# A transformer block on one core: u loaded in eleven pieces, q and k at other distances with high and low parts in turn, Fourier weights by parts, k's token scale by way of HBM

## The chip, the cores and the metric

The kernel runs on one core of one Trainium2 chip, which has eight; the other seven have nothing to do. A core has five engines that run side by side, each through its own list of instructions in the order written: PE (matrix products), ACT (element functions), DVE (element arithmetic), POOL (a slower general engine) and SP, which here only starts transfers. They meet at semaphores. The operands lie in an on-chip memory of 128 partitions; matrix products are summed in banks of a second memory, which ACT and DVE read. The metric is the device time of one execution in microseconds (us), shown as the median of several runs.

## The reference

One encoder layer on x of 256 tokens by 2048 features, in float32:

```
h = RMSNorm(x);  q | k | v | u = h @ w_in
a = RMSNorm(window_attention(q, k, v, sink))      12 query heads, 4 key heads, head width 128,
                                                  |t - s| <= 128, linear bias by distance
f = RMSNorm(fourier_mix(u))                       per group of 128 channels: real part of the 2-D
                                                  transform over (positions, channels), then @ w_fourier
x = x + concat(a, f) @ w_out
g | val = RMSNorm(x) @ w_up
x = x + (GELU(conv3(g)) * val) @ w_down           5504 wide
out = RMSNorm(x)
```

The change touches the stage that makes u, q, k and the Fourier part, so the last three lines concern it only as what comes after.

## The kernel before

Every float32 operand that PE multiplies is split in two: `hi`, the value rounded to a format that PE takes in one pass, and `lo`, what is left. A product is then three passes: hi by hi, lo by hi, hi by lo. A copy on ACT makes `hi`, a subtraction on DVE makes `lo`. Weights come in tiles of 1 MB (`raw`, three buffers), are split into `parts` (three buffers, line 152 on) and used; a split is written two units ahead of its use (`split(i + ahead)`, line 379), and a load three ahead. `PLACES` (line 150) says how many elements into its buffer the hi part and the lo part of each kind of tile begin.

**u.** Norm gain, tokens and u's weights come as one array in 16 pieces, one for each 128 features (k). `U_LOADS` (line 187) groups the pieces into nine loads, four of one piece, four of two and one of four. For each load, `u_weights` splits the weights of the whole load at once and `u_tokens` the tokens of each k; then come six matmuls for each k (`u_products`). ACT and DVE do the work of one load in the order: tokens of the first k, weights of the load, tokens of the other k's.

**Units.** After u the program goes through numbered units, each with one weight tile: 4 to 7 are v, 8 to 23 are q and k (k0, q0, q1, q2, k1, q3 ...), 24 to 39 the output projection. `unit(i, work)` (line 395) runs what is registered to come `before` unit i, the unit's own matmuls, what is registered `beside` it, the split of unit i + 2, and what is registered `behind` it. Every entry is placed by hand with `at(when, i, function)`, so the order of each engine's list follows from this. Beside unit 4 stand the squares of the tokens (`token_sums`, eight on ACT) and the token scale r1; beside unit 5 the rows of u, scaled by r1 and split (`rows_out`), and the split of the position cosines `pos`.

**Fourier part.** `fourier_weights` (before unit 6) multiplies the channel cosines `chan` by the weights `wfs`, both plain float32 (line 490, two products which PE takes as two passes each); `fourier_weights_out` copies the result. `fourier_rows` (before unit 7) multiplies u's rows by pos. From unit 8 to 11, `fourier_channels` joins the two for one group each. `total` sums the squares before unit 14.

**k's token scale.** k is kept with features on the partitions, so its scale r1, one number for each token, is needed as a row repeated on all partitions (`r1b`). Behind unit 6 DVE makes two diagonal matrices of r1; before unit 8 PE multiplies them by ones (line 322); beside unit 8 DVE copies the sum to r1b. `qk_out` of k0, beside unit 9, reads it first (line 602).

**q and k.** A unit makes 128 features of q or k for 256 tokens. `still_weights` (line 344) keeps the weights still and moves tokens: for each of 16 k one matmul of the hi weights with 512 columns (hi and lo of the tokens, line 355) and one of the lo weights with 256 (line 357). `lag` says how many further hi matmuls run ahead of the first lo matmul: q and k use 15, all sixteen hi matmuls and then all sixteen lo ones. The feed-forward part uses 0 (in turn), and 4 for its third tile. `qk_parts` splits the result into `kT` and `qT`. Each head then goes through scores, exponentials, transposes and values in the units that follow.

**The feed-forward part** starts at about 270 us with the same `still_weights` for the first tiles and goes on with three matmuls of 256 columns for each k (`still_thirds`, line 361), and with the down projection as a scheme with fewer products.

Of the kernel before, what the change touches and what calls it, by code (L numbers as in the profile page):

```python
# [8 lines left out]
F32 = mybir.dt.float32  # L9
F32R = mybir.dt.float32r  # L10
AF = mybir.ActivationFunctionType
ALU = mybir.AluOpType

P = 128
D = 2048
S = 256
NK = D // P
# [76 lines left out]
def block_kernel(  # L94
# [18 lines left out]
    nc = tc.nc  # L113
    SL = slopes()
    ctx.enter_context(tc.manual_schedule())
    base = ctx.enter_context(tc.tile_pool(name="base", bufs=1))
    wp = ctx.enter_context(tc.tile_pool(name="wp", bufs=1))
    mm = ctx.enter_context(tc.tile_pool(name="mm", bufs=4, space=bass.MemoryType.PSUM))
    dn = ctx.enter_context(tc.tile_pool(name="dn", bufs=4, space=bass.MemoryType.PSUM))

    def f32(ap):
        return ap.bitcast(F32)

    def bank(pool, name):
        return pool.tile([P, 512], F32, tag=pool.name, name=name)
# [21 lines left out]
    raws, halves = {}, {}  # L147


    PLACES = {"qk": (16, 32), "still": (0, 16), "thirds": (0, 32), "first": (16, 16), "moving": (0, 0), "product": (28, 28)}  # L150

    def parts_tile(name, place):
        t = wp.tile([P, 2 * 2048 + 128], F32R, tag="parts", name=name, bufs=3)
        oh, ol = PLACES[place]
        return t[:, oh : oh + 2048], t[:, 2048 + ol : 4096 + ol]
# [27 lines left out]
    def load_u(k, n):  # L183
        s = slice(NK + k * KS if k else 0, NK + (k + n) * KS)
        nc.sync.dma_start(u_raw[:, s], u_in[:, s])

    U_LOADS = [1, 1, 1, 1, 2, 2, 2, 2, 4]
    for n, size in enumerate(U_LOADS):
        load_u(sum(U_LOADS[:n]), size)
    vec = base.tile([P, V_N], F32, tag="vec", name="vec")  # L190
# [16 lines left out]
    ps = bank(dn, "ps_warm")  # L207
# [3 lines left out]
    def split_scaled(dst, src, g):  # L211

        nc.scalar.activation(dst[:, 0:S], src, AF.Copy, scale=g)
        nc.vector.scalar_tensor_tensor(
            dst[:, S : 2 * S], src, g, f32(dst[:, 0:S]), ALU.mult, ALU.subtract
        )

    hT = []
    for c in range(4):
        t = base.tile([P, 4, 512], F32R, tag=f"hT{c}", name=f"hT{c}")  # L220
# [36 lines left out]
    k = 0  # L257
    for size in U_LOADS:
        if k:
# [12 lines left out]
    cat_pool = pa.enter_context(tc.tile_pool(name="cat", bufs=16))  # L272
    ph = pa.enter_context(tc.tile_pool(name="pa", bufs=1))

    chan = cat_pool.tile([P, 512], F32, tag="cat", name="chan")[:, 0 : 2 * P]
    wfs = cat_pool.tile([P, FW], F32, tag="cat", name="wfs")
# [2 lines left out]
    pos_hi = cat_pool.tile([P, 2, S], F32R, tag="cat", name="pos_hi")  # L279
    pos_lo = cat_pool.tile([P, 2, S], F32R, tag="cat", name="pos_lo")  # L280
    rel = cat_pool.tile([P, 512], F32, tag="cat", name="rel")

    nc.sync.dma_start(chan, c_chan)
    nc.sync.dma_start(wfs, wf)
# [26 lines left out]
    def spread_diagonals(r, name):  # L311
        dgs = []
        for b in range(2):
            dg = base.tile([P, P], F32, tag=f"diag{b}", name=f"diag{name}{b}")
            nc.vector.tensor_scalar(dg, ident, r[:, b : b + 1], None, ALU.mult)
            dgs.append(dg)
        return dgs

    def spread_sums(dgs, name):
        ps = bank(dn, "ps_spread" + name)  # L320
        for b in range(2):
            nc.tensor.matmul(
                ps[:, b * P : (b + 1) * P], ones, dgs[b], start=True, stop=True
            )
        return ps
# [18 lines left out]
    def still_weights(hi, lo, ps, kk, lag=0):  # L344


        todo = [("hi", k) for k in kk[: lag + 1]]
        for n, k in enumerate(kk):
            todo.append(("lo", k))
            todo += [("hi", q) for q in kk[lag + 1 + n : lag + 2 + n]]  # L350
        for part, k in todo:
            h = hT[k // 4][:, k % 4, :]
            s = slice(k * P, (k + 1) * P)
            if part == "hi":
                nc.tensor.matmul(ps, hi[:, s], h, start=k == 0, stop=False)  # L355
            else:
                nc.tensor.matmul(  # L357
                    ps[:, 0:S], lo[:, s], h[:, 0:S], start=False, stop=k == NK - 1
                )
# [26 lines left out]
    before, beside, behind = {}, {}, {}  # L386

    def at(when, i, f, *a):
        when.setdefault(i, []).append((f, a))
# [17 lines left out]
    r1 = base.tile([P, 2], F32, tag="rstd1", name="rstd1")  # L407
# [36 lines left out]
    r1b = ph.tile([P, S], F32, tag="r1b", name="r1b")  # L444
# [3 lines left out]
    at(beside, 5, rows_out, u_hi, u_lo, ps_u)  # L448
    at(behind, 5, query_scales)

    cat = {}

    def feature_out(ps, slot, g, sq, first):
# [25 lines left out]

    held = {}  # L480

    def fourier_positions():
        nc.scalar.activation(pos_hi, pos, AF.Copy)
        nc.vector.tensor_tensor(pos_lo, pos, f32(pos_hi), ALU.subtract)

    def fourier_weights():

        for part in range(2):
            ps = held["g", part] = bank(dn, f"ps_g{part}")
            nc.tensor.matmul(  # L490
                ps, chan[:, part * P : (part + 1) * P], wfs, start=True, stop=True
            )

    def fourier_weights_out():
        for part in range(2):
# [28 lines left out]
    sq_f = ph.tile([P, S], F32, tag="sqf", name="sq_f")  # L524
# [30 lines left out]
            nc.vector.tensor_scalar(rel[:, s], rel[:, s], rq_inv[:, b : b + 1], None, ALU.mult)  # L555
        nc.vector.tensor_scalar(sink_neg, vcol(V_SINK, NH), -1.0, None, ALU.mult)

    spread1 = {}
    at(beside, 5, fourier_positions)
    at(before, 6, fourier_weights)  # L560
    at(beside, 6, fourier_weights_out)
    at(behind, 6, lambda: spread1.update(d=spread_diagonals(r1, "1")))
    at(before, 7, fourier_rows)
    at(beside, 7, fourier_rows_out)
    at(before, 8, lambda: spread1.update(ps=spread_sums(spread1["d"], "1")))
    at(beside, 8, lambda: rows_out(v_hi, v_lo, ps_v))
    at(beside, 8, lambda: nc.vector.tensor_copy(r1b, spread1["ps"][:, :S]))
    at(behind, 8, distances)

    def fourier_channels_steps():  # L570
        for g in range(NG):
            i = 8 + g
            at(before, i, fourier_channels, g)
            at(beside, i, fourier_channels_copy, g)
            at(behind, i, fourier_channels_join, g)
            at(beside, i + 1, fourier_channels_out, g)
        at(before, 14, total, sq_f, "f")
        at(beside, 14, total_scale, "f", FW)


# [12 lines left out]
    qk_sb, st = {}, {}  # L593
# [11 lines left out]
    def qk_parts(kind, h):  # L605

        add = st.pop(("add", kind, h))
        t = ph.tile([P, 512], F32R, tag=f"{kind}T", name=f"{kind}T{h}", bufs=2)
        if kind == "k":
            nc.scalar.activation(t[:, 0:S], add, AF.Copy)  # L610
            nc.vector.tensor_tensor(t[:, S : 2 * S], add, f32(t[:, 0:S]), ALU.subtract)
        else:
            split_scaled(t, add, -1.0 / float(SL[h]))
        qk_sb[kind, h] = t
# [91 lines left out]
    for i in range(N_QK, N_OUT + 8):  # L706
        heads = {i - s: h for (kind, h), s in slot_of.items() if kind == "q"}
        new = [kh for kh, s in slot_of.items() if i - s == 1]
        if 5 in heads:
            at(before, i, values, heads[5])  # L710
        if 4 in heads:
            at(before, i, turn, heads[4])
        if 2 in heads:
            at(before, i, scores, heads[2])
        if 3 in heads:
            at(beside, i, weigh, heads[3])
        for kind, h in new:
            at(beside, i, lambda k=kind, h=h: qk_out(k, h, st.pop(("ps", k, h))))
        if 5 in heads:
            at(beside, i, values_out, heads[5])  # L720
        if 4 in heads:
            at(beside, i, turn_out, heads[4])
        for kind, h in new:
            at(beside, i, qk_parts, kind, h)
        if 2 in heads:
            at(beside, i, scores_out, heads[2])
            at(behind, i, exps, heads[2])

    fourier_channels_steps()
    for n, (kind, h) in enumerate(QK_ORDER):  # L730

        def work(hi, lo):
            ps = st["ps", kind, h] = bank(mm, f"ps_{kind}{h}")
            still_weights(hi, lo, ps, range(NK), lag=NK - 1)

        unit(N_QK + n, work)

# [49 lines left out]
    for n, (c, kq) in enumerate(OUT_ORDER):  # L787
        i = N_OUT + n
# [14 lines left out]
        if kq >= 2:  # L803
            part = "a" if kq == 2 else "f"
            ps = ps_a[c] if kq < 3 else ps_a[c, "f"]
# [312 lines left out]
    for q in range(2):  # L1118
        kind, j = items[q]
        ps = bank(mm, f"ps_{kind}{j}")  # L1120
# [16 lines left out]
    for n, it in enumerate(items):  # L1137
# [8 lines left out]
        if it[0] in ("gate", "val"):  # L1146
            kind, j = it
            ps = bank(mm, f"ps_{kind}{j}")
# [7 lines left out]
        if it[0] == "product":  # L1156
            kind, g, c, p = it
            hi, lo = halves.pop(it)
            both = c == 2
            shape = (2, 1024) if both else (4, 512)  # L1160
            for cc in (0, 1) if both else (c,):
                o = 512 * cc if both else 0
                if (cc, p) in held:
                    first, end = (g, c) == FIRST_SET[cc], (g, c) == LAST_SET[cc]
                    by_parts(held[cc, p], parts[p], hi, lo, first, end, *shape, o)
                    continue
                ps = bank(mm, f"ps_{p}{g}{cc}")
# [6 lines left out]
        else:  # L1174
            kind, g, c = it
            hi, lo = halves.pop(up_index[n])
            ps = [bank(mm, f"ps_l{g}{c}{b}") for b in range(2)]
# [10 lines left out]
    i = up_index[n]  # L1188

    def split_last(c):  # L1190
        raw, n = raws[i + c], 512 * len(LAST)
        o = PLACES["product"][0]
        hi, lo = halves[i + c] = [
# [144 lines left out]
```

## Time and profile before

| what | us |
|---|---|
| median of three runs | 947.99 |
| lowest, highest | 947.69, 948.75 |
| the profiled execution | 947.65 |
| its span in the profile | 945.9 |
| PE busy | 936.6 |
| DVE busy | 711.2 |
| ACT busy | 535.7 |
| POOL busy | 47.2 |

The span runs from the first to the last record, 1.75 us less than the execution's own time. The profile gives for each engine when each instruction began and how long it took, with the tiles that it wrote and read and the line of the program; the note in brackets is how long the engine sat idle before, and what released it. An instruction merged over several has an x with their number. PE's matmuls overlap, so the time of one is longer than its share of the stream: the distance from one start to the next is what counts. PEld is the loading of weights into the array, ahead of the matmul that uses them. PEclk is the granted clock of PE as a share of full speed. In the chain of waits, each piece is a stretch of the work that ended last, and its lengths add up without overlap.

### The profile page before, as it was taken

What the parts mean: (1) busy time and instruction counts of PE and PEld (TensorE: products, weight loads), DVE (VectorE), ACT (ScalarE), POOL (GpSimd) and SP (SyncE); (2) the same over time, 40 slices, a digit from 0 to 9 for tenths busy, and PEclk for the clock granted to TensorE, in tenths of its full rate; (3) what the DMA queues carried; (4) which work ended last, traced back from release to release, by engine and by line L of the source; (5) the groups of instructions that cost most, each with busy time, mean ns of one, the idle gap of its engine ahead of it and who ended that gap; (6) DMA issues with size and microseconds to landing.
All of it is one profiled execution on the core that took longest, in us unless ns stands there. A gap on an engine that the chain in (4) does not pass through costs nothing.

```text
span 945.9 us, 15007 instructions
## 1 busy us (share of the span) xinstructions
PE 936.6 (99%) x6277; PEld 858.0 (91%) x6277; DVE 711.2 (75%) x816; ACT 535.7 (57%) x620; POOL 47.2 (5%) x62
## 2 busy tenths in 40 slices
PE   9999999999999999999999999999999999999996
PEld 7889899888888899999999999999999999999985
DVE  6658877666667776769676887768878678889695
ACT  7656666544465555546555555555555555655544
POOL 0000000000000000000000000000000000000003
PEclk9999999999999999999999999999999999999998
DMA  9844534455559687577888778787878987769742
GB/s 365 332 166 160 178 135 153 158 179 181 185 215 299 199 256 227 190 252 223 267 239 257 244 248 266 249 278 224 265 234 239 290 262 248 242 222 261 227 181 89
DMA packets 32260, 214.87 MB, mean 227 GB/s; under 512 B 3520, under 2 KB 3776, under 8 KB 7744
## 3 DMA queue, kind: packets, MB, share of 16 engines
q1 hardware_dynamic: 28160, 184.55, 53.4%
q0 software_dynamic: 4032, 29.36, 16.2%
q8 instruction: 49, 0.80, 0.3%
q14 instruction: 19, 0.16, 0.0%
HBM read 211.80 MB, written 2.10 MB: 226 GB/s over the span
## 4 chain that ended last, share of the span: by engine, by line
PE 96%; DMA 2%; SPq 0%; ACT 0%; DVE 0%; issue 0%; POOL 0%; ACTq 0%; POOLq 0%
PE ps_val L368 22%; PE ps_gate L368 21%; PE ps_q L355 5%; PE ps_P L1061 3%; PE ps_P L1060 3%; PE ps_P L1059 3%; PE ps_N L1060 3%; PE ps_N L1061 3%; PE ps_N L1059 3%; PE ps_q L357 2%; PE ps_a L340 2%; PE ps_a L338 2%; PE ps_a L339 2%; PE ps_gate L355 2%; PE ps_val L355 2%; PE ps_k L355 2%
## 5 line engine op out<-in xcount | busy, mean ns | idle before, releaser
L171 DVE TENSOR_TENSOR parts<-raw,parts 128x2048 fp32r<-128x2048 f32 (+1 forms) x129 | 293.4, 2274 | 70.8 <-ACT parts L170 70.6
L170 ACT ACTIVATE parts<-raw 128x2048 fp32r<-128x2048 f32 (+1 forms) x129 | 245.9, 1906 | 79.5 <-PE ps_gate L368 19.9
L368 PEld LDWEIGHTS ps_val<-hU,parts 128*128 128x128 f32 x1824 | 211.6, 188 | 2.2
L368 PE MATMUL ps_val<-hU,parts 128*128 128x256 f32 x1824 | 212.9, 276 | 0.0
L368 PEld LDWEIGHTS ps_gate<-hU,parts 128*128 128x128 f32 x1776 | 206.4, 188 | 2.5
L368 PE MATMUL ps_gate<-hU,parts 128*128 128x256 f32 x1776 | 207.3, 276 | 0.0
L836 ACT ACTIVATE fa_v<-ps_val 128x256 f32<-128x256 f32 x38 | 14.6, 384 | 88.4 <-PE ps_val L368 88.2
L946 DVE TENSOR_TENSOR parts_N<-sumw,parts_N 128x2048 fp32r<-128x2048 f32 x18 | 41.2, 2290 | 21.2 <-ACT parts_N L945 21.1
L1059 PE MATMUL ps_P<-parts_P,op_P 128*128 128x512 f32 x144 | 56.0, 389 | 0.0
L1061 PE MATMUL ps_P<-parts_P,op_P 128*128 128x512 f32 x144 | 56.0, 389 | 0.0
L1060 PE MATMUL ps_P<-parts_P,op_P 128*128 128x512 f32 x144 | 56.0, 389 | 0.0
L355 PE MATMUL ps_q<-hT,parts 128*128 128x512 f32 x192 | 46.3, 393 | 0.0
L945 ACT ACTIVATE parts_N<-sumw 128x2048 fp32r<-128x2048 f32 x18 | 34.4, 1913 | 14.3 <-PE ps_gate L368 10.6
L1061 PE MATMUL ps_N<-parts_N,op_N 128*128 128x512 f32 x108 | 42.0, 389 | 0.0
L1059 PE MATMUL ps_N<-parts_N,op_N 128*128 128x512 f32 x108 | 42.0, 389 | 0.0
L1060 PE MATMUL ps_N<-parts_N,op_N 128*128 128x512 f32 x108 | 42.0, 389 | 0.0
L355 PEld LDWEIGHTS ps_q<-hT,parts 128*128 128x128 f32 x192 | 35.2, 188 | 6.9
L338 PE MATMUL ps_a<-parts,cat 128*128 128x512 f32 x96 | 37.9, 394 | 0.0
L340 PE MATMUL ps_a<-parts,cat 128*128 128x512 f32 x96 | 37.5, 390 | 0.0
L339 PE MATMUL ps_a<-parts,cat 128*128 128x512 f32 x96 | 37.4, 389 | 0.0
L946 DVE TENSOR_TENSOR parts_P<-sumw,parts_P 128x2048 fp32r<-128x2048 f32 x9 | 20.6, 2289 | 16.6 <-ACT parts_P L945 16.6
L355 PE MATMUL ps_gate<-hU,parts 128*128 128x512 f32 x96 | 32.7, 390 | 0.0
(343 smaller groups left out, 1492.0 us busy)
## 6 DMA issues: line engine op xcount, KB each, us to landing
raw<-in_w_up SPq DMA_DIRECT2D x86, 1024.0 KB, 5.9
raw<-in_w_in SPq DMA_DIRECT2D x20, 1024.0 KB, 4.9
sumw<-in_w_down POOLq DMA_DIRECT2D x18, 1024.0 KB, 8.5
raw<-in_w_out SPq DMA_DIRECT2D x16, 1024.0 KB, 4.9
raw<-in_w_down_late SPq DMA_DIRECT2D x4, 1024.0 KB, 6.2
u_raw<-in_u_in SPq DMA_DIRECT2D x4, 768.0 KB, 9.1
raw<-in_w_down_last SPq DMA_DIRECT2D x4, 768.0 KB, 4.4
xs<-in_x SPq DMA_DIRECT2D x4, 512.0 KB, 17.3
```

The costliest lines, as they stand in the source:

```text
L170: nc.scalar.activation(hi, raw, AF.Copy)
L171: nc.vector.tensor_tensor(lo, raw, f32(hi), ALU.subtract)
L338: nc.tensor.matmul(ps, ah, wh, start=first and q == q0, stop=False)
L339: nc.tensor.matmul(ps, al, wh, start=False, stop=False)
L340: nc.tensor.matmul(ps, ah, wl, start=False, stop=last and q == q0 + len(kk) - 1)
L355: nc.tensor.matmul(ps, hi[:, s], h, start=k == 0, stop=False)
L368: nc.tensor.matmul(ps[:, 0:S], w[:, s], h[:, o : o + S], start=k == 0 and n == 0, stop=k == NK - 1 and n == 2,)
L945: nc.scalar.activation(hi, src, AF.Copy)
L946: nc.vector.tensor_tensor(lo, src, f32(hi), ALU.subtract)
L1059: nc.tensor.matmul(ps, o[:, 0, p, :], hi[:, s], start=first and p == 0, stop=False)
L1060: nc.tensor.matmul(ps, o[:, 1, p, :], hi[:, s], start=False, stop=False)
L1061: nc.tensor.matmul(ps, o[:, 0, p, :], lo[:, s], start=False, stop=end)
```

## The change

Six edits, all in the first 170 us of the span:

- u comes in eleven loads: six of one piece, five of two.
- The hi part of a q or k tile begins 32 elements into its buffer in place of 16, the lo part 80 in place of 32. Units alternate between a lead of four hi matmuls (8, 10, ...) and strictly in turn (9, 11, ...).
- `chan` and `wfs` are split on ACT and DVE beside unit 5, after u's rows and ahead of pos; `fourier_weights` becomes three one-pass matmuls for each of its two products.
- r1 is written by POOL's queue to a row in HBM, behind unit 5, and read back to all partitions as r1b. The diagonals, their two products and the copy go.
- A small tile of 16 elements is set aside after the first `kT`, so that `qT` and what is allocated after it lie 64 bytes further on.
- The call that places `total` before unit 14 stands in another loop.

```diff
-    PLACES = {"qk": (16, 32), "still": (0, 16), "thirds": (0, 32), "first": (16, 16), "moving": (0, 0), "product": (28, 28)}
+    PLACES = {"qk": (32, 80), "still": (0, 16), "thirds": (0, 32), "first": (16, 16), "moving": (0, 0), "product": (28, 28)}
...
-    U_LOADS = [1, 1, 1, 1, 2, 2, 2, 2, 4]
+    U_LOADS = [1] * 6 + [2] * 5
...
+    chan_hl, wfs_hi, wfs_lo = (
+        cat_pool.tile([P, 512], F32R, tag="cat", name=n) for n in ("chan_hl", "wfs_hi", "wfs_lo")
+    )
...
+    def key_scales():
+
+        row = dram.tile([1, S], F32, tag="row", name="row1")
+        nc.gpsimd.dma_start(row[0].rearrange("(b p) -> p b", p=P), r1)
+        nc.gpsimd.dma_start(r1b, row[0].partition_broadcast(P))
+
+    at(behind, 5, key_scales)
...
+    def fourier_parts():
+        for t, lo in ((chan_hl[:, 0 : 2 * P], chan_hl[:, 2 * P :]), (wfs_hi, wfs_lo)):
+            src = chan if lo is not wfs_lo else wfs
+            nc.scalar.activation(t, src, AF.Copy)
+            nc.vector.tensor_tensor(lo, src, f32(t), ALU.subtract)
...
-            nc.tensor.matmul(
-                ps, chan[:, part * P : (part + 1) * P], wfs, start=True, stop=True
-            )
+            for n, (o, w) in enumerate([(0, wfs_hi), (2 * P, wfs_hi), (0, wfs_lo)]):
+                a = chan_hl[:, o + part * P : o + (part + 1) * P]
+                nc.tensor.matmul(ps, a, w, start=n == 0, stop=n == 2)
...
-    spread1 = {}
+    at(beside, 5, fourier_parts)
     at(beside, 5, fourier_positions)
     at(before, 6, fourier_weights)
     at(beside, 6, fourier_weights_out)
-    at(behind, 6, lambda: spread1.update(d=spread_diagonals(r1, "1")))
     at(before, 7, fourier_rows)
     at(beside, 7, fourier_rows_out)
-    at(before, 8, lambda: spread1.update(ps=spread_sums(spread1["d"], "1")))
     at(beside, 8, lambda: rows_out(v_hi, v_lo, ps_v))
-    at(beside, 8, lambda: nc.vector.tensor_copy(r1b, spread1["ps"][:, :S]))
     at(behind, 8, distances)
...
-        at(before, 14, total, sq_f, "f")
...
+        if not qk_sb:
+
+            ph.tile([P, 16], F32, tag="pad", name="pad")
...
+        if i == 14:
+            at(before, i, total, sq_f, "f")
...
-            still_weights(hi, lo, ps, range(NK), lag=NK - 1)
+            still_weights(hi, lo, ps, range(NK), lag=0 if n % 2 else 4)
```

More of the change, by code (lines that the diff above doesn't have):

```diff
@@ L117, in block_kernel @@
     wp = ctx.enter_context(tc.tile_pool(name="wp", bufs=1))
+    dram = ctx.enter_context(tc.tile_pool(name="dram", bufs=1, space=bass.MemoryType.DRAM))
     mm = ctx.enter_context(tc.tile_pool(name="mm", bufs=4, space=bass.MemoryType.PSUM))
```

## The prediction

> **What bounds the kernel now.** I read the page's totals and chain of waits first.
>
> ```profile
> span 945.9 us, 15007 instructions
> ...
> PE 96%; DMA 2%; SPq 0%; ACT 0%; DVE 0%; issue 0%; POOL 0%; ACTq 0%; POOLq 0%
> ```
>
> 96% of the chain lies on PE, so a microsecond taken off PE's stream, or a hole torn into it, is a microsecond of the span. The change ends before the feed-forward part begins at about 270 us, and it moves no operand of the matmuls that come after; what has been gained or lost by then is carried to the end. So I work out when PE gets through each stage. Next comes the timeline of ACT and DVE around the place where the Fourier weights are used.
>
> ```profile
> 27.93 1.92 ACT L170 ACTIVATE parts<-raw 128x2048 fp32r<-128x2048 f32 x1 [3.62 <-DMA raw<-in_w_in]
> ...
> 29.76 0.61 ACT L307 ACTIVATE junka<-xs 128x512 f32<-128x512 f32 x1
> ...
> 35.65 1.91 ACT L170 ACTIVATE parts<-raw 128x2048 fp32r<-128x2048 f32 x1
> ...
> 37.46 1.24 ACT L431 ACTIVATE u_hi<-ps_u,rstd 128x512 fp32r<-128x512 f32 x2
> ...
> 38.59 0.63 ACT L483 ACTIVATE pos_hi<-pos 128x512 fp32r<-128x512 f32 x1
> ...
> 39.11 1.91 ACT L170 ACTIVATE parts<-raw 128x2048 fp32r<-128x2048 f32 x1
> ...
> 37.59 2.29 DVE L171 TENSOR_TENSOR parts<-raw,parts 128x2048 fp32r<-128x2048 f32 x1 [1.45 <-ACT parts L170]
> ...
> 39.80 1.40 DVE L432 SCALAR_TENSOR_TENSOR u_lo<-ps_u,rstd,u_hi 128x512 fp32r<-128x512 f32 x2
> ...
> 41.12 0.68 DVE L484 TENSOR_TENSOR pos_lo<-pos,pos_hi 128x512 fp32r<-128x512 f32 x1
> ```
>
> ACT waits 3.62 us for the weights of unit 5, which arrive at 27.93, and then has no gap: split of unit 5, eight token sums (29.76 to 35.65), split of unit 6, the high rows of u at 37.46, those of pos at 38.59. DVE follows: low part of unit 6 until 39.88, low rows of u until about 41.15, low part of pos. This string hangs on one transfer and not on PE. PE at the same place:
>
> ```profile
> 39.24 1.88 PE L490 MATMUL ps_g<-wfs,chan 128*128 128x512 f32 x4
> ...
> 41.19 0.40 PE L339 MATMUL ps_v<-parts,hT 128*128 128x512 f32 x1
> ```
>
> The four plain-f32 passes of L490 start at 39.24. The second matmul of unit 6 starts at 41.19, so the unit itself starts one matmul of 0.23 earlier, at 40.96. L490 needs only two transfers that were there long before.
>
> **The change part by part.** *The loads of u.*
>
> ```profile
> 5.11 5.79 PE L253 MATMUL ps_u<-parts,hT 128*128 128x512 f32 x24
> ...
> 18.99 0.51 ACT L213 ACTIVATE hT<-u_raw 128x256 fp32r<-128x256 f32 x1 [1.82 <-DMA u_raw<-in_u_in]
> ...
> 21.34 2.29 DVE L242 TENSOR_TENSOR parts<-u_raw,parts 128x2048 fp32r<-128x2048 f32 x1 [1.32 <-ACT parts L241]
> ...
> 23.68 4.41 PEld L253 LDWEIGHTS ps_u<-parts,hT 128*128 128x128 f32 x20 [0.50 <-DVE parts L242]
> ...
> 28.14 0.19 PEld L338 LDWEIGHTS ps_v<-parts,hT 128*128 128x128 f32 x1
> ```
>
> The last load brings four k at once, its low part is ready at 23.63, and 20 matmuls are left for the 4.46 us to 28.14 (0.223 each). With pieces of two, the low part of the last pair is ready near 22 while PE is still behind it: 96 x 0.223 = 21.4 us from 5.11, with some 0.4 us of early waits, ends at 27.0, about 1.15 us earlier. Units 4 and 5 (28.14 to 39.24) then end at 38.0 in place of 39.2. The price is smaller transfers, seen in the table by stretch (last figures: DMA share, GB/s):
>
> ```profile
> 4.00:8.00 4.00, 4.00 (x21) 3.37 (x20) 3.15 (x7) 2.73 (x6) 0.00 (x0) 1.00 1.03 363
> 8.00:16.00 8.00, 7.67 (x33) 5.71 (x33) 6.91 (x11) 7.11 (x13) 0.00 (x0) 1.00 1.02 418
> ```
>
> Single pieces went at 363 GB/s, pairs at 418; two more singles (0.79 MB) cost 0 to 0.29 us in front of every later transfer, the one of 27.93 included. I take 0.15.
>
> *Fourier weights by parts.* fourier_parts stands behind the rows of u and ahead of pos, on both engines. A 512-wide split costs what pos shows, 0.63 and 0.68; the 256-wide one of chan is nearest to this row:
>
> ```profile
> 63.17 0.43 DVE L611 TENSOR_TENSOR kT<-add_k,kT 128x256 fp32r<-128x256 f32 x1 [0.49 <-ACT kT L610]
> ```
>
> ACT has both high parts by about 39.6. DVE starts chan's low part at 41.12, has it at 41.55 and that of wfs at about 42.15. PE, which is in order, has been standing at these matmuls since 38.0: one can go at 39.6, the next at 41.55, and four are left at 42.2. These take 4 x 0.23 = 0.9, so unit 6 starts at 43.1 instead of 40.96: **+2.15**. Everything that the finer loads gave is waited away in here, because the string behind 27.93 has not moved. Behind PE wait only unit 6 and what follows it; split 7 and 8 on ACT and DVE move by about 1 us and are used at 46.4 and later. If the parts were ready in time, six matmuls of 0.23 (1.38) would replace 1.72 (40.96 less 39.24), which bounds this edit from below; from above, DVE could be late by one more 2048-wide split (2.3).
>
> *k's token scale.* The two matmuls of L322 go (0.44, next fence), and two short DVE operations. In their place stand two transfers from POOL, which has nothing else to do there. The nearest is POOL's broadcast of normf_g; this line is its time to landing, and the row behind it the first reader of r1b:
>
> ```profile
> DMA to landing us min/median/max: 12.4/12.4/12.4
> ...
> 62.26 0.43 DVE L602 TENSOR_TENSOR add_k<-add_k,r1b 128x256 f32<-128x256 f32 x1
> ```
>
> r1 is there before 37.46; two transfers in a row end by 37.5 + 2 x 12.4 = 62.3 even at that pace. The reader comes some 1.7 us later than now, and the first transfer carries 1 KB. I take zero; were the cover gone, DVE's k rows would wait, and PE only for the first scores at 73. **-0.44**.
>
> *q and k: order and distances.* From the chain:
>
> ```profile
> 54.91 0.44 PE ps_spread L322 x4
> ...
> 55.80 3.66 PE ps_k L355 x16
> 59.46 1.89 PE ps_k L357 x16
> ...
> 73.39 0.72 PE ps_s L621 x6
> ...
> 157.60 3.63 PE ps_q L355 x16
> ...
> 271.46 1.16 PE ps_gate L355 x5
> ...
> 276.95 0.23 PE ps_val L355
> ```
>
> One of the sixteen units takes 3.66 + 1.89 = 5.55 us, all high parts and then all low ones. The gate tile at 271.46 does the same matmuls with a lead of five and takes 276.95 - 271.46 = 5.49. Tiles strictly in turn:
>
> ```profile
> 282.23 0.39 PE L355 MATMUL ps_gate<-hU,parts 128*128 128x512 f32 x1
> ...
> 287.67 0.39 PE L355 MATMUL ps_val<-hU,parts 128*128 128x512 f32 x1
> ```
>
> From the first matmul of one tile to the first of the next that is 5.44. Eight units get the lead of five, eight none: 8 x 0.06 + 8 x 0.11 = **-1.4**. What (32, 80) does as a distance no row shows. The best row bounds the gain at 16 x 0.11 = 1.8; if high and low went at the 0.12 per 256 columns of the scores (0.72 for six), a unit would take 16 x 0.36 = 5.76, a loss of 3.4. I take the FFN's pace, the nearest row, which has yet other distances. Low parts are early enough to be used at once: one is made at 78.70 for matmuls at 87.35.
>
> ```profile
> 78.70 2.29 DVE L171 TENSOR_TENSOR parts<-raw,parts 128x2048 fp32r<-128x2048 f32 x1 [0.63 <-ACT parts L170]
> ```
>
> *q 64 bytes on.* Scores run at 0.12; at the 5.44/48 = 0.113 of the tiles in turn, a head saves 0.04, twelve 0.5. Zero is as likely; **-0.25**. The step of `total` is no change: unit 14 has no scores, so the list ahead of it stays values, turn, total.
>
> *The clock.* PE now has no hole over 0.5 us. The new hole runs from 38.0 to 42.2 with two matmuls in it.
>
> ```profile
> 937.68 0.28 PE L1209 MATMUL ps_e<-lo,act 128*128 128x256 f32 x1
> ```
>
> ```profile
> 940.00:942.00 2.00, 0.00 (x0) 0.00 (x0) 1.09 (x2) 1.27 (x2) 0.00 (x0) 0.55 0.35 135
> ```
>
> ```profile
> 0.99 4.36 PE L209 MATMUL ps_warm<-ones 128*128 128x128 f32 x20 [0.99 <-POOL ones L201]
> ```
>
> The last matmul ends at 937.96. The mean clock of 0.55 after 940 means a fall to half at about 940.2, that is 2.2 us of idleness. At the start 20 matmuls took 4.36 us (0.218 each), against 0.11 for the same form in L322: half rate for some 4 us of work before the full clock came. So I expect the hole to cost the clock for up to 4 us after it, 0 to 2.0 us of time; I take **+1.6**, since part of that stretch will lie in the hole.
>
> The Trainium skill (TensorE: Matmul & The Clock Gate, Part 1: The HAM clock gate) states that the half rate comes after at least one idle window of about 3.4 us. By that rule a hole broken up by two matmuls keeps the clock, and the sum would lack the 1.6. The fall after 2.2 us of idleness fits it only if the window counted as idle still held some work.
>
> **Sum**, against the profiled execution's 947.65: +0.15 + 2.15 - 0.44 - 1.4 - 0.25 + 1.6 = +1.8. The median shown, 947.99, is 0.34 above that execution; on it the forecast is **949.8**.
>
> **Rivals.** (1) *The hole is there, the clock holds*, because two matmuls inside it count as work: +0.2, 948.2. For: neither idle piece is over 2 us (38.0 to 39.6, 39.8 to 41.55). Against: the fall 2.2 us after the end. That is the page's rule, worked as a mechanism here. (2) *The parts are there in time*, because ACT's string gets free earlier than I hold: then 1.15 + 0.34 + 0.44 + 1.4 + 0.25 = 3.6 are gained, 944.4. For: nothing but the arrival at 27.93 holds it. Against: bytes and order ahead of that transfer are unchanged. (3) *The distances are bad*: with (32, 80) units run at 5.76 or between that and 5.55. From 5.6 on the gain turns to a loss; half of the bound of 3.4 lost in place of 1.4 won gives +3.1 on top of (1): 951.3, slower. For: the pace does differ between rows of one shape (0.113, 0.118, 0.12). Against: the order in turn reached 5.44 on other distances.
>
> **Numbers.** Forecast 0.46, (1) 0.24, (2) 0.19, (3) 0.11. This kernel's measurement can tell about 0.2%, 1.9 us, from no change, so 946.1 to 949.9 counts as the same. The forecast lies on that edge: half of it slower (0.23), half the same (0.23). With (3) slower is 0.34; with (1), less 0.01 for its own tail, the same is 0.46; with (2) and that tail faster is 0.20. The likeliest case alone has 948.4 to 951.4 (clock 0.2 to 2.0, units as bounded by 5.44 and 5.55). The range 944.5 to 951.6 takes in that, (1), and half of (2) and of (3).
>
> **What will show it.** Right: PE waits for DVE's wfs_lo near 42, unit 6 starts near 43; unit 4 starts near 27; q and k units of 5.45 to 5.5; a granted clock under 1 for the stretch from 42 to 46. Wrong: no wait of PE on fourier_parts (then 2); a clock of 1.00 there (then 1); units longer than 5.55 (then 3); DVE waiting for r1b.

## The result, and the profile after

The changed kernel takes **952.05 us** (median of 5 runs, 951.78 to 952.56) against 947.99 (by now five runs of the kernel before, with the same median): the ratio is 1.0042, 95% interval 1.0028 to 1.0057. It is slower by 4.1 us, and 0.45 us above the top of the predicted range. The profiled execution took 952.56.

The page's totals and its chain of waits:

```profile
span 950.8 us, 15019 instructions
...
PE 94%; DMA 3%; ACT 1%; issue 0%; DVE 0%; SPq 0%; POOL 0%; ACTq 0%; POOLq 0%; DVEq 0%
```

Two of the 96% that lay on PE have gone to a DMA, ACT and DVE. The chain itself, in order of time (start, duration, engine, output, line), says where:

```profile
12.34 15.96 DMA raw<-in_w_in
28.41 1.92 ACT parts L171
...
36.22 1.82 ACT parts L171
38.07 1.18 DVE parts L172
...
40.27 0.32 DVE u_lo L436
...
40.94 0.74 DVE u_lo L436
41.68 0.33 DVE chan_hl L498
42.01 0.61 DVE wfs_lo L498
42.67 1.20 PE ps_g L510 x4
43.87 0.41 PE ps_v L342
44.28 0.43 PE ps_v L343
...
46.84 0.43 PE ps_v L343
47.27 0.24 PE ps_v L344
...
50.96 2.88 PE ps_f L528 x24
...
59.72 1.17 PE ps_k L359 x5
...
65.34 0.44 PE ps_y L547 x4
```

Up to 42.67 the program hangs on the string that starts with unit 5's weights at 28.41: splits, rows of u, then the parts of the Fourier weights. What PE itself waited for, in the view of waits by engine (engine, tile and line, releaser: us in total, times, longest):

```profile
PE ps_g L510 <- DVE chan_hl L498: 1.5, 1, 1.5
PE ps_g L510 <- ACT wfs_hi L497: 1.1, 1, 1.1
```

Then unit 6's first nine matmuls stand about 0.43 apart in place of 0.23. The view by stretch (PE, PEld, DVE, ACT and POOL busy with counts, granted clock, DMA share, GB/s) has the reason:

```profile
36.93:40.34 3.41, 2.33 (x11) 1.53 (x9) 2.27 (x2) 3.41 (x6) 1.40 (x2) 1.00 0.59 236
40.34:43.76 3.42, 1.80 (x7) 1.10 (x7) 3.42 (x7) 2.54 (x3) 0.00 (x0) 1.00 1.27 53
43.76:47.17 3.41, 3.41 (x10) 2.67 (x9) 1.97 (x4) 1.64 (x3) 0.35 (x1) 0.50 0.75 31
```

The clock was granted at half rate from 43.76 to 47.17, just after the hole. The sum of the differences along PE's stream (40.96 is worked out as in the prediction, as the second matmul's 41.19 less 0.23):

| stretch | before | after | difference |
|---|---|---|---|
| first matmul of unit 6 | 40.96 | 43.70 | +2.74 |
| unit 6, from the end of ps_g to its own end | 5.47 | 7.09 | +1.62 |
| four matmuls of L322 | 0.44 | none | -0.44 |
| the 16 q and k units, sum | 88.87 | 89.78 | +0.91 |
| scores and values of all twelve heads, sum | 17.16 | 16.91 | -0.25 |
| last matmul's end | 937.96 | 942.49 | +4.53 |

The five terms give 4.58. Behind the last matmul the profiled execution has another 0.4 us more than the one of before, 8.30 against 7.92 (run 6 shows what brings them); the medians differ by 4.06.

k's token scale by way of HBM cost nothing. POOL's two issues, and the time that the second took to land:

```profile
37.73 0.91 POOL L458 DMA_DIRECT2D row<-rstd  x1 [0.32 <-POOL rstd L306]
46.82 0.59 POOL L459 DMA_DIRECT2D r1b<-row  x1 [8.18 <-DMA row<-rstd]
```

```profile
r1b<-row POOLq DMA_DIRECT2D x1, 128.0 KB, 7.1
```

r1b is there at 46.82 + 7.1 = 53.9, and DVE first turns to k at 65.80; it shows no wait for it.

### The profile page after: what moved, and what is told of

The parts are those of the page before. It is cut to its first block, busy times and chain, and to the rows that moved or that the text cites. A ratio compares the mean times of both kernels' runs of the same rounds, so it can differ in the third digit from the quotient of the medians.

```text
span 950.8 us, 15019 instructions
## 1 busy us (share of the span) xinstructions
PE 938.8 (99%) x6275; PEld 859.8 (90%) x6275; DVE 711.9 (75%) x817; ACT 537.3 (57%) x624; POOL 48.2 (5%) x64
## 4 chain that ended last, share of the span: by engine, by line
PE 94%; DMA 3%; ACT 1%; issue 0%; DVE 0%; SPq 0%; POOL 0%; ACTq 0%; POOLq 0%; DVEq 0%
PE ps_val L372 22%; PE ps_gate L372 21%; PE ps_q L359 5%; PE ps_P L1080 3%; PE ps_P L1079 3%; PE ps_P L1078 3%; PE ps_N L1080 3%; PE ps_N L1079 3%; PE ps_N L1078 3%; PE ps_q L361 2%; PE ps_a L344 2%; PE ps_a L343 2%; PE ps_a L342 2%; PE ps_gate L359 2%; PE ps_val L359 2%; DMA raw<-in_w_in 2%
## 5 line engine op out<-in xcount | busy, mean ns | idle before, releaser
L359 PE MATMUL ps_q<-hT,parts 128*128 128x512 f32 x192 | 66.3, 397 | 0.0
L361 PE MATMUL ps_q<-hT,parts 128*128 128x256 f32 x192 | 51.3, 281 | 0.0
L359 PEld LDWEIGHTS ps_q<-hT,parts 128*128 128x128 f32 x192 | 35.8, 188 | 7.6
L361 PEld LDWEIGHTS ps_q<-hT,parts 128*128 128x128 f32 x192 | 35.5, 189 | 0.3
```

The costliest lines, as they stand in the source:

```text
L361: nc.tensor.matmul(ps[:, 0:S], lo[:, s], h[:, 0:S], start=False, stop=k == NK - 1)
```

## The experiments

Times are medians, ratios are against the kernel before measured in the same series (947.82 for runs 1 to 4, 947.74 for runs 5 to 8, 947.90 for runs 9 to 11), with 95% intervals.

**1. Plain Fourier weights, the rest of the change kept.**

```diff
-    at(beside, 5, fourier_parts)
...
-            for n, (o, w) in enumerate([(0, wfs_hi), (2 * P, wfs_hi), (0, wfs_lo)]):
-                a = chan_hl[:, o + part * P : o + (part + 1) * P]
-                nc.tensor.matmul(ps, a, w, start=n == 0, stop=n == 2)
+            nc.tensor.matmul(ps, chan[:, part * P : (part + 1) * P], wfs, start=True, stop=True)
```

> The changed kernel with chan and wfs as plain float32 again, no fourier_parts. Theory (the hole in front of unit 6 is made by waiting for chan's and wfs's low parts): PE goes from unit 5 at 39.0 straight into the four plain passes (1.72), unit 6 starts at 40.7 and the clock holds; 3.0 + 1.6 = 4.6 us less than the changed kernel, about 947.4. Rival (the hole only moves, because unit 6's own low part or the rows of u are late as well): unit 6 still starts after 42, and no more than 1 us is gained, 951.

947.50 us, ratio 0.9995 [0.9986, 1.0005]: 4.55 less than the changed kernel, or 4.4 when each is taken against the kernel before of its own series. One row of the chain shows it; ps_f, which follows unit 6, started at 50.96 above:

```profile
45.97 2.88 PE ps_f L528 x24
```

The hole is gone, and the clock is held (0.998 over the run). The Fourier parts alone make the change a loss.

**2. The hole filled.** Fourteen products of ones with ones are put in front of the parts' matmuls.

```diff
+        hold = bank(dn, "ps_hold")
+        for _ in range(14):
+            nc.tensor.matmul(hold[:, 0:P], ones, ones, start=True, stop=True)
```

> The changed kernel with 14 products of ones by ones (about 3.1 us, nobody reads them) put into the hole. Theory (the clock fell because PE stood): the waits stay, the clock holds, unit 6 takes 5.45 in place of 7.09: 1.6 us less, about 950.4. Rival (the slow unit 6 has another cause than idleness): unit 6 stays at 7.1 and the time at 952 or, with the fillers in the way, a little over.

950.62 us, ratio 1.0031 [1.0020, 1.0041]: 1.43 less than the changed kernel, with more work. The chain:

```profile
39.12 3.12 PE ps_hold L508 x28
42.24 1.38 PE ps_g L513 x6
...
49.10 2.88 PE ps_f L531 x24
```

Unit 6 runs from 43.62 (42.24 + 1.38) to 49.10, in 5.48 us: full clock. The parts come no sooner for it: the fillers (28 passes) end at 42.24, and DVE has the last part ready at about 42.15. So the loss of 4.4 to 4.55 has two pieces, about 1.5 of clock and 3 of waiting.

**3. Distances back to (16, 32).**

```diff
-    PLACES = {"qk": (32, 80), ...
+    PLACES = {"qk": (16, 32), ...
```

> The changed kernel with the q and k parts at (16, 32) again, order in turn kept. Theory (the distances made the units slow): units of 5.45 to 5.50 in place of 5.61, 16 x 0.13 = 2.1 us less, about 950.0. Rival (the order in turn made them slow): units stay at 5.6, 952.

951.28 us, ratio 1.0036 [1.0023, 1.0049]. The units take 5.55 to 5.57, 89.02 in sum: 0.76 less than with (32, 80), not the 2.1 expected. The order in turn is not worth 0.06 to 0.11 a unit at these distances; it is worth nothing (88.87 before). A second thing was not expected: in this profile the clock held, although the same hole is there.

```profile
37.65:41.06 3.41, 1.92 (x8) 1.02 (x6) 2.59 (x2) 3.41 (x7) 1.09 (x2) 1.00 0.52 206
41.06:44.48 3.42, 1.91 (x7) 1.39 (x8) 3.42 (x6) 2.45 (x3) 0.00 (x0) 1.00 1.54 58
44.48:47.89 3.41, 3.41 (x17) 2.78 (x16) 1.66 (x4) 0.42 (x1) 0.00 (x0) 1.00 0.58 24
```

These stretches were laid out backward from this run's own fall of the clock at its end, 945.60, in steps of 3.413 us (the last section says why). The hole is split more evenly between two of them. The five executions of this kernel have mean clocks between 0.994 and 0.998, so the clock was lost in some and not in others, and the sums of the units say more here than the median.

**4. Order back, distances kept at (32, 80).**

```diff
-            still_weights(hi, lo, ps, range(NK), lag=0 if n % 2 else 4)
+            still_weights(hi, lo, ps, range(NK), lag=NK - 1)
```

> The changed kernel with all sixteen high parts first again, distances (32, 80) kept. Theory (the distances made the units slow): units stay at 5.6 or above, 952 or more. Rival (the order made them slow): units of 5.55 as before the change, 16 x 0.06 = 1.0 us less, about 951.1.

952.45 us, ratio 1.0045 [1.0030, 1.0060]. The chain, for the same unit that took 3.66 + 1.89 before:

```profile
59.17 3.74 PE ps_k L359 x16
62.91 1.91 PE ps_k L361 x16
```

5.65; the sixteen units take 90.39. With before's 88.87, run 3's 89.02 and the change's 89.78 the four corners are there: the distances cost 1.52 in the old order and 0.76 in the new; the new order costs 0.15 at (16, 32) and gives 0.61 at (32, 80).

**5. Parts made earlier**, behind unit 4, so that they do not wait for the rows of u.

```diff
-    at(beside, 5, fourier_parts)
+    at(beside, 4, fourier_parts)
```

> The changed kernel with fourier_parts behind unit 4 in place of unit 5: its four instructions stand ahead of the split of unit 6 and of the rows of u. Theory (the loss at unit 6 is only the order on ACT and DVE): the six ps_g matmuls follow unit 5 at once and take 1.4, unit 6 starts near 40.4 instead of 43.7, the clock holds, and 3.3 + 1.6 = 4.9 are won back: a span of 945.9, time 947.2. Rival (chan and the Fourier weights arrive too late for this place, near 34, so that the token scales, split 6 and the rows of u slip behind them): half of it is lost again as a wait of PE in unit 6 or at ps_f, time 949.5.

947.79 us, ratio 1.0000 [0.9990, 1.0009]. The wait at ps_g is gone and the clock holds, as the theory said, but the chain shows where the rival was half right:

```profile
36.71 1.81 ACT parts L171
38.55 2.30 DVE parts L172
40.89 0.51 PE ps_v L344
...
46.19 2.88 PE ps_f L528 x24
```

Split 6 now stands behind two more instructions on ACT, its low part is ready at 38.55 + 2.30 = 40.85, and the third matmul of unit 6 lasts 0.51 on the chain where one takes 0.23. The first product of the Fourier weights started at 38.83 here and at 38.63 in run 1, and unit 6 ends at 46.19 and 45.97: 7.36 and 7.34. The parts take 1.37 on PE against 1.72, and the wait for split 6 takes it back: their four small instructions on ACT and DVE stand in a string that has no slack.

**6. The eleven loads alone**, in the kernel before.

```diff
-    U_LOADS = [1, 1, 1, 1, 2, 2, 2, 2, 4]
+    U_LOADS = [1] * 6 + [2] * 5
```

> The kernel before with the eleven loads of u only. Theory (the loads bring unit 4 forward by 0.43, the weights of unit 5 come 0.48 later, and with plain Fourier weights nothing on PE waits for these): unit 6 ends about 0.4 earlier, time 947.6. Rival (the later arrival decides): PE waits in unit 5 or 6, time 948.4.

947.47 us, ratio 0.9997 [0.9987, 1.0006]: by itself too little to measure. In its profile unit 4 starts at 27.34, against 28.36 before, and all of that second is still there at ps_f (45.56, against 46.58):

```profile
38.38 1.72 PE ps_g L490 x4
45.56 2.88 PE ps_f L510 x24
```

Unit 5's weights came at 27.79 here. Over all ten profiles with eleven loads they came between 27.57 and 28.81, on average at 28.17; over three with nine loads at 27.74, 27.93 and 28.16, on average 27.94. The 0.2 between the means is not clear of this scatter, so a price of the loads for later transfers isn't shown. Unit 4 scatters as well: it starts between 27.34 and 28.07 in the ten profiles, on average at 27.73, and between 28.36 and 28.57 in the three, on average at 28.50.

The profiled execution is quicker by 0.63 only, 947.02 against 947.65, though its last matmul ends 1.03 earlier, at 936.93. The rest is lost behind that matmul: 8.31 us to the end of the span, against 7.92. All ten profiles with eleven loads have 8.30 to 8.32 there, the three with nine 7.92 to 7.94. In the traces SP ends with a row of waits on semaphores; with nine loads the wait that is over last, 7.04 us behind the last matmul, closes the row, and with eleven loads the one that is over at 7.05 has six more behind it, 0.06 us each.

**7. q and k at the feed-forward distances**, in the kernel before, with the new order.

```diff
-    PLACES = {"qk": (16, 32), ...
+    PLACES = {"qk": (0, 16), ...
...
-            still_weights(hi, lo, ps, range(NK), lag=NK - 1)
+            still_weights(hi, lo, ps, range(NK), lag=0 if n % 2 else 4)
```

> The kernel before with the q and k parts at (0, 16), the distances that the feed-forward tiles have, and leads of 4 and 0 in turn. Theory (the distance of the parts sets the pace of these matmuls, and (0, 16) has the feed-forward part's pace): the sixteen units take 5.44 to 5.50 each, 87.0 to 88.0 in sum against 88.87 before, and the time is about 946.5. Rival (the feed-forward tiles are quick for another reason, and the distance does not matter): 5.55 as before, 88.9, time 948.0.

947.72 us, ratio 1.0000 [0.9991, 1.0010]; sum 88.65. Neither theory: eight units take 5.44 to 5.48, and eight 5.60 or 5.61 (5.70 for unit 14, which has about 0.1 more than its pace asks for in every kernel, behind the sums of the Fourier features). The distance alone does not set the pace.

**8. A scan**: each unit of the kernel before at another pair of distances, in the old order.

```diff
+    SCAN = {f"parts{8 + n}": p for n, p in enumerate([(0, 16), (8, 24), (16, 32), (24, 40), (32, 48), (40, 56), (48, 64), (56, 72), (32, 80), (64, 96), (80, 112), (96, 128), (0, 64), (0, 0), (16, 80), (32, 32)])}
...
-        oh, ol = PLACES[place]
+        oh, ol = SCAN.get(name, PLACES[place])
```

> The kernel before with another pair of distances in each of the sixteen q and k units, all high parts first and then all low ones as before, so that the interval of the high matmuls belongs to the first distance and that of the low ones to the second. Theory (the distance sets the pace): high near 228 ns and low near 118 at (16, 32), about 233 at a first distance of 32 and 119 at a second of 80, and other places between 227 and 234 and between 113 and 120. Rival (something else that the change moves sets it): all units at 228 and 118 within 1.5 ns whatever the distance.

948.45 us, a single run. The chain's rows for (0, 16), (16, 32), (32, 80) and (0, 64), two each, high and then low:

```profile
56.01 3.69 PE ps_k L357 x16
59.69 1.90 PE ps_k L359 x16
...
68.10 3.66 PE ps_q L357 x16
71.76 1.89 PE ps_q L359 x16
...
109.67 3.73 PE ps_k L357 x16
113.40 1.90 PE ps_k L359 x16
...
137.58 3.66 PE ps_k L357 x16
141.25 1.82 PE ps_k L359 x16
```

The theory holds as far as places differ (5.48 to 5.66 a unit, where the old place gave 5.52 to 5.58 but for unit 14 in both), and (32, 80) is among the slow ones. But (0, 16), the feed-forward place, is slow here, at 5.59, and the old order reaches 5.48 at (0, 64) and (0, 0).

The starts of the single matmuls in the trace say more. Once settled, the high ones come 226, 229 and 232 ns apart by turns where the first distance is 0 or 64 (units 8, 17, 20, 21), 226 or 227 apart at 16 or 80 (units 10, 18, 22), and about 231 and 236 by turns at 32 or 96 (units 12, 16, 19, 23). So in this order their pace goes by the first distance, whatever the unit, and comes back 64 elements further on. For the low ones the theory failed: second distances of 64 gave 113.4 ns at (0, 64) and 117.9 at (48, 64).

**9. What is left of the change without its two bad parts**: eleven loads, HBM, q 64 bytes on; Fourier weights, distances and order of before.

```diff
-    PLACES = {"qk": (32, 80), ...
+    PLACES = {"qk": (16, 32), ...
...
-            still_weights(hi, lo, ps, range(NK), lag=0 if n % 2 else 4)
+            still_weights(hi, lo, ps, range(NK), lag=NK - 1)
```

(on top of the edit of run 1)

> The changed kernel with plain Fourier weights and with before's distances (16, 32) and before's order; what is left of the change are the eleven loads, the token scale by way of HBM, q 64 bytes on and the later place of one sum. Theory (the three parts that helped add up): 0.4 to 1.0 from the loads, 0.44 from L322, 0.2 from the scores, so 1.0 to 1.6 less than before: 946.1 to 946.7. Rival (the q and k units react to what stands between them, so that other scores change their pace too): units off 5.55 by more than 0.03 at the same distances and order, and a time that differs from that by up to 0.7 either way.

946.74 us, ratio 0.9987 [0.9978, 0.9996]. The three parts add up to 1.16. The units keep to 5.52 to 5.58 but for unit 14 (5.67), sum 88.84 against 88.87 before: single units move by up to 0.04, but at these distances and in this order the sum does not react to the other scores.

**10 and 11. The same with (0, 16)**, leads of 4 and 0 in turn, and strictly in turn.

```diff
-    PLACES = {"qk": (16, 32), ...
+    PLACES = {"qk": (0, 16), ...
...
-            still_weights(hi, lo, ps, range(NK), lag=NK - 1)
+            still_weights(hi, lo, ps, range(NK), lag=0 if n % 2 else 4)
```

> As the run without the Fourier parts, but q and k at (0, 16), leads of 4 and 0 in turn: the same sixteen units as in the run of before at the feed-forward distances, with other scores (64 bytes on) between them. Theory (a unit falls into one of two paces, 5.44 or 5.61, by what stands ahead of it, and keeps it to its end): again no unit between 5.50 and 5.58, but another list of quick ones than 9, 11, 12, 13, 16, 17, 20 and 21; sum 87.0 to 89.7, time 945.0 to 947.7. Rival (the pace belongs to a unit's own operands and buffers, which are the same): the same list, sum 88.65, time 946.5.

946.11 us, ratio 0.9981 [0.9972, 0.9990]; sum 88.26. The last line of the diff becomes `lag=0` in run 11:

> The same with strictly high and low in turn in all sixteen units. Theory (entry decides): eight units begin otherwise than in the run with leads of 4 and 0, so the list of quick units changes once more, also among the units that had no lead there; sum 87.0 to 89.7. Rival (the lead decides): all sixteen alike, 5.44 each (87.0, time 944.9) or 5.61 each (89.7, time 947.6).

**945.97 us, ratio 0.9980 [0.9971, 0.9989]**; sum 87.95. This is the quickest kernel of the study, 1.9 us under the one before and 6.0 under the change, each against the kernel before of its series. Its units 17 and 18, first and last rows on the chain with what stands between them:

```profile
114.08 0.23 PE ps_q L359
...
119.54 0.71 PE ps_o L709 x6
120.25 0.44 PE ps_t L687 x4
120.69 0.23 PE ps_q L359
...
126.29 0.71 PE ps_o L709 x6
```

The same 32 matmuls at the same distances take 119.54 - 114.08 = 5.46 in one unit and 126.29 - 120.69 = 5.60 in the next. All lengths in us, each from the end of the group ahead of the unit to its own end:

| kernel | units 8 to 23 | sum |
|---|---|---|
| before: (16, 32), high first | 5.55 5.58 5.58 5.56 5.54 5.55 5.66 5.52 5.55 5.54 5.56 5.52 5.54 5.54 5.56 5.52 | 88.87 |
| after: (32, 80), 4 and 0 | 5.62 5.60 5.51 5.46 5.62 5.65 5.72 5.63 5.61 5.63 5.61 5.63 5.61 5.63 5.62 5.63 | 89.78 |
| run 3: (16, 32), 4 and 0 | 5.57 5.57 5.56 5.55 5.55 5.56 5.67 5.55 5.54 5.56 5.57 5.55 5.54 5.56 5.57 5.55 | 89.02 |
| run 4: (32, 80), high first | 5.65 5.64 5.63 5.64 5.65 5.64 5.76 5.64 5.65 5.63 5.65 5.64 5.65 5.63 5.65 5.64 | 90.39 |
| run 7: (0, 16), 4 and 0 | 5.61 5.48 5.61 5.47 5.48 5.44 5.70 5.60 5.48 5.44 5.61 5.60 5.48 5.44 5.61 5.60 | 88.65 |
| run 10: (0, 16), 4 and 0 | 5.50 5.60 5.49 5.48 5.49 5.60 5.59 5.46 5.48 5.46 5.49 5.60 5.48 5.60 5.48 5.46 | 88.26 |
| run 11: (0, 16), in turn | 5.48 5.60 5.48 5.48 5.46 5.46 5.57 5.46 5.46 5.46 5.60 5.46 5.46 5.46 5.60 5.46 | 87.95 |

Runs 7 and 10 have the same operands in their units and other scores between them, and the list of quick units changes from 9, 11, 12, 13, 16, 17, 20, 21 to 8, 10, 11, 12, 14, 15, 16, 17, 18, 20, 22, 23, as run 10's theory said (unit 14 with its 0.1 counts by the pace of its matmuls). Run 11 changes the list again, also among the odd units, which are strictly in turn in both: 13, 19 and 21 are slow in run 10 and quick in run 11, as its theory said. It is not the luck of one execution: the changed kernel and runs 1, 2 and 5 have the same q and k stage, and their profiles agree to 0.01 in all sixteen units. So a unit's own distances and order don't settle its pace. They settle which paces there are; what is around the unit settles which of them it falls into. Whether that is what stands ahead of it or what runs beside it was not separated, since nothing was changed in front of one unit alone.

## Why the prediction was wrong

**The Fourier parts: right.** ACT and DVE got to them when the prediction said, behind the rows of u. The stops are as foretold, one matmul at 40.05, one at 42.07, four behind; PE waited for wfs_hi of ACT and chan_hl and wfs_lo of DVE, and unit 6 began at 43.70 for a foretold 43.25 (43.1 and the 0.15 for later transfers). Of the 0.45 between them 0.33 is the arrival, 28.41 in this profile in place of 28.08, and 0.1 that the last four matmuls took 1.03 in place of 0.9. Run 1 takes the whole away. Rival (2) was tried by run 5: parts in time take 1.37 on PE, as its bound of 1.38 had it, but what this saves is lost again at the low part of split 6.

**The clock: right in place, and its size in part luck.** +1.6 was foretold and +1.62 measured, and run 2 shows that filling the hole wins it back. But the prediction thought of up to 4 us at half rate, some of it inside the hole, and what came was one stretch of 3.41 us, all of it behind the hole. The Trainium skill (TensorE: Matmul & The Clock Gate, Part 1: The HAM clock gate) asks for an idle window; the step before the fall had seven matmuls and 1.80 us of PE in it, so here the measurement decides against that wording. Rival (1) happened in one profile, that of run 3, and by its time and mean clock in one further execution, of run 4 (last section), while all five of the changed kernel have a mean clock of 0.995 or 0.996: the 1.6 was likely and not certain.

**The loads, L322 and the scores: right in kind, the loads too large in size.** The loads' gain was waited away in the hole, as foretold; without the hole it comes out, but the sign "unit 4 starts near 27" did not show: 27.93 in this profile, 27.73 on average, a gain of 0.8 and not 1.15. Nor is all that is gained by 270 us carried to the end: the loads cost 0.4 behind the last matmul, which the prediction put at nothing (run 6). L322's 0.44 is in every profile of the change. The scores gave 0.18 for 0.25, and the values behind them another 0.09.

**q and k: the step that failed.** The prediction took -1.4 from "order and distances", and +0.91 came: an error of 2.3, without which the time would have been within the range. That 949.8 + 2.3 = 952.1 is just the median measured is luck: in the profiled executions the forecast is short by 3.1 (4.91 for 1.8), which is this 2.3, 0.4 for unit 6's start and 0.4 behind the last matmul, and the medians happen to take the last two away. Two things were wrong in the step. First, 5.55 and 5.44 were read as the price of the order, because the rows compared differed in order; they differed in distance, too, and in what stands between the units. At (16, 32) the order gives nothing (run 3). Second, (32, 80), of which no row told anything, was taken as neutral, and it costs 0.8 to 1.5 (runs 3 and 4). At (0, 16) the order in turn brings most units to 5.46 or 5.48 and others to 5.60 (run 11), so even there 5.44 is not a price of the order. Rival (3) named this loss, but it was priced on top of a clock that holds (and its turn from gain to loss, put at 5.6 a unit, is 5.55 by the row of before). The range left out that the forecast's clock and rival (3) come together, though nothing tied the one to the other. By its own bounds (clock 0.2 to 2.0, units 5.44 to 5.55) the likeliest case runs from 948.0 to 951.6, not from 948.4 to 951.4.

The medians, each against the kernel before of its own series, close the account: the three parts that help give -1.16 (run 9); with distances and order it is -0.32 (run 1), so these cost 0.84; with the Fourier parts it is +4.06, so these cost 4.38.

## What to carry to other kernels

Before work is moved from a full engine to two that look half idle, look at when their string gets free at that place: ACT and DVE are busy for 57% and 75% of this run, but here they were the late ones. A hole in PE's stream can be paid twice, by its length and by 3.4 us at half clock behind it. And the pace of back-to-back matmuls can differ by 2 to 3% with the places of their operands and with what stands between them: measure the combination that will run, not one factor from a neighbouring stage.

## What the runs showed of the hardware

**The clock is judged on a grid that is fixed within a run.** Every rise and fall in these profiles is a multiple of 3.413 us from the others of its run: in the changed kernel the full clock came at 6.21, left at 43.76 (11 steps later), came back at 47.17 (1 step) and left at 944.88 (263 steps). Where the grid lies differs from run to run, the first rise coming between 4.20 and 6.95. By the rows' busy time the clock was lost after steps in which PE had worked for 1.80 us or less (1.80 in the changed kernel; 0.72 in run 4), and kept through steps with 1.91 and 1.92 (run 3) and with 1.50 and 1.78 at the end of runs 8 and 11. In run 4:

```profile
38.54:41.96 3.42, 0.72 (x2) 0.37 (x2) 3.42 (x5) 3.42 (x5) 0.00 (x0) 1.00 1.44 77
41.96:45.37 3.41, 3.41 (x8) 2.47 (x8) 3.38 (x6) 1.23 (x3) 0.00 (x0) 0.50 0.47 24
```

And in run 8:

```profile
937.25:940.66 3.41, 1.50 (x13) 1.30 (x12) 1.54 (x6) 1.74 (x6) 2.15 (x3) 1.00 0.40 154
940.66:944.08 3.42, 0.00 (x0) 0.00 (x0) 1.15 (x2) 1.33 (x2) 0.04 (x1) 1.00 0.59 220
```

These bounds cross (the ends of matmuls are modelled, and what counts as work isn't shown), but if busy time decides, they put the limit near half of a step, far from an idle one. So the same hole seems to cost 1.6 us or nothing by where the grid falls. Of run 4's four executions three took 952.37 to 952.62 us at a mean clock of 0.996, and one took 950.71 at 0.998; a step at half rate is 0.0018 of the span. Run 3's go from 949.78 (0.998) to 953.04 (0.994), which is more than one step explains. That it is the grid and not something else that spared these executions is argued from these rows; no run moved the grid alone. The Trainium skill (TensorE: Matmul & The Clock Gate, Part 1: The HAM clock gate) calls the window free-running and the cold count variable with its phase, and the trace agrees: the first rise came anywhere from 4.20 to 6.95.

**Matmuls lock into one of a few paces.** The starts in a unit at (0, 16) settle within the first ten matmuls at 226 or 227 and 113 or 114 ns (512 and 256 columns), or at 232 or 233 and 117 or 118, and the unit keeps this as long as high and low alternate, in all sixteen units of runs 7, 10 and 11 (in units with a lead most of the four low parts left over at the end take 116 to 120). At (32, 80), with leads of 4 and 0, 14 of 16 units stay near the slow pace, at about 232 and 118; at (16, 32) all of them lie between, near 229.5 and 117. With all high parts first the high ones settle at 226.7 and the low ones at 117.7 at (16, 32), and at about 233.3 and 119.4 at (32, 80). Why is not known.
